# A hybrid encoder layer on one core: the router's search in a fixed order, and another issue order for everything before it

## The chip, the cores and the metric

The kernel runs on one core of a Trainium2 chip. The core has five engines that work at the same time and meet only through semaphores: TensorE (PE, matmuls; PEld is its weight load), VectorE (DVE), ScalarE (ACT), GpSimd (POOL) and SyncE (SP, which here only issues DMAs). The metric is the device time of one execution in microseconds (us), as the median of repeated runs.

## The reference

One layer of a bidirectional encoder on x of 1024 tokens x 1024 channels, in fp32. What is computed, in short:

```python
n = rms_norm(h, norm1_w)
proj = n @ w_in                                  # 1024 x (4608 conv + 2048 gate + 64 scalar) columns
c = silu(centred_dwconv(conv_in, conv_w, conv_b))  # 7 taps along the sequence
q, k, v, xs, Bm, Cm = split(c)
o_gdn = rms_norm(gated_delta_fw + gated_delta_bw) * silu(g_gate)      # 8 heads of 128, chunks of 64
y = ssd_fw + ssd_bw + D * x_ssd                  # Mamba-2 style, 16 heads of 64, 2 groups
y = rms_norm(y * silu(z))
h = h + concat([o_gdn, y]) @ w_out

n = rms_norm(h, norm2_w)
aff = softmax(n @ w_router)                      # 1024 tokens x 16 experts
vals, idx = top_k(aff.T, 128)                    # every expert chooses 128 tokens
xs = n[idx]
y = (silu(xs @ w_gate) * (xs @ w_up)) @ w_down * vals     # 16 experts, hidden width 512
h = h + scatter_add(y at idx)
out = rms_norm(h, final_norm_w)
```

## The kernel before, in words

The program is one long sequence of small jobs. Each job is a Python function that issues a few instructions on one or two engines; a job with `yield` in it is issued in pieces. Every job is entered with `at(slot, function, ...)`. `flush("mixer")` then issues the 3602 pieces of the mixer (everything up to the router's logits), in the order of a table of numbers, `ORDER["mixer"]`, and `flush("moe")` issues the experts, sorted by slot. Within an engine the instructions run in the order in which they were issued. Both flushes stand under `tc.manual_schedule()`, where that order is kept. The block of code between them, which holds the router's choice of tokens, does not: there a scheduler decides the order, and it may put an instruction of this block among those of the mixer or of the experts.

Matmuls of fp32 data are made from three passes: each operand is split into a high part (a rounded copy, made on ACT) and the rest (a subtraction, on DVE), and hi x hi, hi x lo and lo x hi are added up in PSUM. In the rows `whi` and `wlo` are the two parts of a projection weight, and `n` is a tile of activations or of output weights.

The stages, in order of time:
- RMSNorm and transposes of x, up to about 40 us. ACT copies the transposed x, scaled by a column of gains, out of PSUM (`n<-g,cols`); DVE makes the rest. `Rf` is a small tile in which the decay rates of the heads are prepared with an Exp.
- The input projection in units of 128 columns (`w_unit`, L242; `w_half`, L250), with the convolution of each unit, and under it the 8 gated-delta heads (DVE, POOL and ACT beside PE).
- The two SSD groups, about 770 to 940 us: per head a decay matrix E is made, POOL subtracts (`E<-E,tb_gc`) and masks it (L560), ACT takes its Exp, DVE multiplies it, POOL adds up and PE uses it (L1118). `xw` is an input that is weighted on POOL.
- The output projection in 6 rounds (L1289). At the end of a round `o_end` adds the product to the residual on DVE (`n<-pj,n`).
- The router's logits (L1326, L1335), which end in `lg` on DVE.
- The choice of tokens, in the block under no manual schedule. Softmax: Exp of `lg` on ACT, sum and reciprocal on DVE, `aff`. Then 15 rounds that fix the 128th largest affinity of every expert, two bits a round: DVE compares all affinities with three trial thresholds (`msk<-aff,trial`), PE counts them with a matrix of ones (`c`, L1533), DVE picks the largest threshold that still has at least 128 (`best`, L126, then L1537) and makes the next trials. Then the positions of the chosen tokens (L1543 to L1565), and per expert eight one-hot tiles (`oh`, job `rt`), from which PE collects the token numbers and their weights (`aux`, L1580); POOL issues the gather of the expert's 128 rows (`place<-n2D,idx`, L1591).
- In the gaps of the 15 rounds the first expert's six weight tiles are split: ACT makes the high parts (`place<-place`, six at once), DVE the rests, 12 halves of 128 x 512.
- 16 experts (`L1648`, `L1664`, `L1667`, `L1612`), their weights streamed from HBM through a pool of buffers; a tail with the final norm.

An Exp and a Silu belong to different function tables of ACT. `warm` is a 128 x 1 dummy on which the kernel calls a function early, so that its table (`ACT_TABLE_LOAD`) is there when it is needed: an Exp of `warm` in the last output round, and a Silu of `warm` right behind the Exp of `lg` in the source.

Of the kernel before, what the change touches and what calls it, by code (L numbers as in the profile page):

```python
# [55 lines left out]
        "7Qg}c3kPK`5*ET@QA{06FP5FyI*nce!$cry87zb0dO2uqG-|6y=#e_C9-@Z|aim`iONHeSSC7*1bbOsaJ3UTM&>3|?ok*{M6);+pPAt!?gz=*A"
        "dKIjKF?zgS4I#|YNpw;jUMJII^>V#TuYrl8<a#Yk(i!wRSO+O|N?|3eg%x_T^y^`zUZrR0^)N+G)f4pw*Z|Y?CfEeiHS2P^tSFVvrB~}2dZykC"
        "X=QV^o~<(rIrK)IMQ77%^jf*uC~ScZdXvtov+H#_r=F)f>-jpJUZ6v6wm@#ZS#Oay=GJ+Hj(V<MsPpRbdc8iOE9iW3UZfZ6PI6kJkLazsu->M("
        ">m543E~pDgUq}}bP6<WzQk_Zf(p_~oeN=bXU4&!$xK6K&>Eikjl+b5%DV<vAA*VCCq?}9Z0;Y^U3<XV3-Ak9zm342?QK+JK>m!iQ9EFN9k3wZ#"
        "MOW3;^c8(xyt>dwpVfP$tFF)K8p1_gN#{5DO)XtZ_tiD^1!-#Qf~JhADbHNedvzgG*zA+8j!;_{F-1*1y<Z>DJM~H7pgygOnd0WOuBYqkL;A9Q"  # L60
        "sjo_^D_qmp^$mSf-_j*aDO1`s&><>m>gz_PvAM19=)1bCX{7Jz`}&P;s1NH#;^oW({ZN-Tk96Z870fGL(LB~qbQ9sJZW^SS(8N?T)y;F=)RZ;N"
        "bqG)OGyPtF)6ew_UCF%Ae@qMALbuctOl4EWw9?IFzqxs@Kj{zpqpo49nii&|X=PgKw&t^LC7WM#dh=F))iG6TUCY!q-}QIhTDQ?PO-=Jd|Ik16"
        "UpciC(i&xc>3|8CP^PsGWq#|n!XMpU|I=+uYx7!C2MuP3sbks(Q#+$gdpUQ|{q#F+3>s@fn+~R<31jM-dZxZ1(@*!;VNE*YO()aYbTQ7bX<!<f"
        "0cK#Z9VTQn1M~nL-efZ2g$QPl86iGU57Z+h4K@)?B$GiHX-1juX0#b2T57_X%qEL$Wi=junQZ2_Y(<vc?Bd-_6!Ed*(Zq9@uBL~HDml98DSJ^("
        "PDw+B#U_UE&-60AO)T@*tPt;G#+mVEqM2kAM#9)8gvn-#nQ8zv{*~V*BB90TCZ^EWOf%EX3=_vV>}O`0S!TB6cqXo4oMYyShr;+64-;TK6F*33"
        "41<g1ex8|c7MK7AFd;_4geHUp!V<GkSY*OtBFTv`9EO*a*hIi(CMrh7#F*IhmvclcgR4yvOp2S#YV*=0HAzHkOk_-n$uKfT!z3n|u-2?I>*Xf7"
        "u)%B;Phno0l;Ww(F|*P{$5m#tu*D?Dlp#HCG26{nv(4<3jnqO6Ok>iRRJhyhFuTki6BC!4)Ob{$-edNeG?MnpeJ<gZ*>4J90nBX<m{^zxV`ChQ"
        "i)rzQd1DTlbeJCVVkSIj4x7B@h{=HY@Rd1kGGi9ZYu=i7rVySs@6GApJR{^0^2)P2ut<<?_`#er`SGLqB=fxaEc#-KVlga%7t94y9M6jmVOBhA"
        "zM4y>Bn}tfj@vOCUN)D_F5HcKa4()PC*|(4$&NYjl(}Ngnw*#mOW{tuXwHf6!^3#RTr;JyEMCBCrkuQ|JXXMpSV=Z2<9<AV*Ufd48?Ty!SOu$M"
        "HOwf_TsJq&G3joY!gvI$V-37zZsARHTjp&eQ>cl@@dVz%lUNIDV;!uE1+g$574Dde*g*WQxhK@cdU#jvPT~EK2Jg$fZyw-7Y=Wn;5iZ3?_`p0g"  # L70
        "&9OP2!L!&9&tnT|+Q~Z}nMbBRKE+meQQEt*^;l?$t+76~!M505xP(tkQ|usq8K0RB*cCftN9->7x#@(B@i7j>=Vl;w!H1?B_P{5iLHNQ9!hhHk"
        "ui#_z)cnC_I9Sfl@HxJ~<@f`iO8dg}!rs_NcE6c^conbVbsU1<%u9TQeX&2@z-4$-Gyq>?7drso;2#_=ti%xl+MhTIf8l#vC37@>H$Q~oxEhDy"
        "P&tng*5C@^r}>Rw!LF6|rx}Oi<n$IhS!es%@$y&rJNzI&l2GzUVI8i=4YFtDzO!_(ZEU*{C*VgMD|EKq>;#-7OvK69)lL?lh@bE;cDGZ|+s~-%"
        "7bMFzV0%at%7(VnWN#`?!=83JPQ`@wD}KZ2@<cD&+s?o~c7W|`!`QGkoDFXy*v7WMFvt#;?HM==huDZVl8tPm*lAYTs5Y97W2f6uHi3<9W7wF&"
        "Oq^k7;Y^&3L+xygW#`~PJJ1f3Ia}J%cC?*`^Kh;()6T_Ic9tD(N7&gmv5hNAX6IuPQA4``N7^}du1zW_xm|=~>{vU`e#iNeQ`nR?wQP+QPb0*$"
        "8Etwy&W^VW>_WT9F2=<e$ELOEY+hjr=Ck>1W}CrgvRQ;3b|Egr#lg7*<J%>6f}Loa*gSTU>~6v)c9+d>m)b-&o1{H<vdwOD*iE<@x7ckqtDRzV"
# [1757 lines left out]
```

## Time and profile before

| | |
|---|---|
| runs | 1676.93, 1672.53 and 1685.21 us, median 1676.93 |
| profiled execution | 1671.89 us; span of its trace 1670.2 us |
| mean granted TensorE clock | 0.972 |
| PE busy | 1550.8 us (93%) |
| DVE busy | 1211.5 us (73%) |
| ACT busy | 982.0 us (59%) |
| POOL busy | 730.0 us (44%) |
| DMA | 254.20 MB, mean 152 GB/s |

The profiled execution is 5.0 us below the median of the runs, and 0.6 us below the lowest of them. Busy shares are means over stages that differ: PE is near its limit in the projections, POOL in the SSD stage, DVE in the router's rounds, and the DMA engines in most of the experts' stage.

### The profile page before, as it was taken

How to read it: one execution, taken by the hardware profiler on the slowest of the kernel's cores; microseconds unless marked ns; L12 is line 12 of the kernel's file. 1: busy time of each engine (PE TensorE's matmuls, PEld its weight loads, DVE VectorE, ACT ScalarE, POOL GpSimd, SP SyncE). 2: the span in 40 equal slices, each digit the busy share in tenths (PEclk: the TensorE clock that was granted, in tenths of full speed). 3: DMA queues.
4: the chain of work that ended last, by engine and by line, in shares of the span. 5: the costliest groups of instructions: out<-in, count | busy, mean ns of one | idle time of the engine just before them, and what ended most of it. 6: DMA issues, size and time to landing. Idle time of an engine off the chain costs nothing. (4 is left out here: it accounts for less than half of the span.)

```text
span 1670.2 us, 23559 instructions
## 1 busy us (share of the span) xinstructions
PE 1550.8 (93%) x8290; PEld 1264.7 (76%) x8290; DVE 1211.5 (73%) x2045; ACT 982.0 (59%) x1788; POOL 730.0 (44%) x533
## 2 busy tenths in 40 slices
PE   5989999999999999998989999998996499899997
PEld 4768888888889888887765687687885377677774
DVE  4686768686767677757779976864556598789875
ACT  5476485858586767465542574243455177677764
POOL 1285263647454654425898877713032011111112
PEclk9999999999999999999999999999997599999999
DMA  4322223223231322222332245457787289999955
GB/s 137 98 60 43 45 65 68 75 56 87 42 98 28 105 70 63 39 70 95 108 101 70 67 135 172 150 183 263 256 284 291 111 311 372 329 382 375 389 184 213
DMA packets 174784, 254.20 MB, mean 152 GB/s; under 512 B 54370, under 2 KB 112027, under 8 KB 174667
## 3 DMA queue, kind: packets, MB, share of 16 engines
q1 hardware_dynamic: 170202, 236.45, 42.3%
q0 software_dynamic: 4464, 16.25, 3.8%
q8 instruction: 65, 1.06, 0.3%
q14 instruction: 53, 0.43, 0.1%
HBM read 221.01 MB, written 31.65 MB: 151 GB/s over the span
## 5 line engine op out<-in xcount | busy, mean ns | idle before, releaser
L242 PE MATMUL pj<-n,whi 128*128 128x512 f32 x1664 | 482.5, 412 | 9.8 <-ACT whi L129 7.5
L242 PEld LDWEIGHTS pj<-n,whi 128*128 128x128 f32 x1664 | 301.0, 190 | 79.2 <-ACT whi L129 11.1
L242 PE MATMUL pj<-n,wlo 128*128 128x512 f32 x832 | 263.4, 398 | 3.6 <-DVE wlo L123 3.5
L123 DVE TENSOR_TENSOR place<-place 128x1024 fp32r<-128x1024 f32 (+1 forms) x182 | 208.0, 1184 | 27.8 <-ACT place L129 27.8
L126 DVE SCALAR_TENSOR_TENSOR cacc<-pj,cols,cacc 128x1023 f32<-128x1023 f32 (+2 forms) x156 | 199.3, 1278 | 22.8 <-POOL cacc L123 20.1
L123 POOL TENSOR_TENSOR cacc<-cacc,cpr 128x1021 f32<-128x1021 f32 x60 | 145.7, 2429 | 153.4 <-ACT cacc L129 81.0
L1648 PE MATMUL pj<-place 128*128 128x512 f32 x768 | 198.3, 410 | 2.0 <-DVE place L123 1.3
L129 ACT ACTIVATE place<-place 128x1024 fp32r<-128x1024 f32 (+1 forms) x181 | 181.5, 1053 | 16.8 <-issue 8.5
L242 PEld LDWEIGHTS pj<-n,wlo 128*128 128x128 f32 x832 | 156.2, 189 | 45.8 <-DVE wlo L123 8.3
L1648 PEld LDWEIGHTS pj<-place 128*128 128x128 f32 x768 | 144.5, 192 | 40.6 <-DVE place L123 5.3
L123 DVE TENSOR_TENSOR n<-n 128x1024 fp32r<-128x1024 f32 x64 | 84.3, 1327 | 68.9 <-ACT n L129 40.7
L1591 POOL DMA_INDIRECT place<-n2D,idx x16 | 17.4, 1088 | 259.4 <-ACT place L129 93.7
L129 ACT ACTIVATE n<-n 128x1024 fp32r<-128x1024 f32 x64 | 66.7, 1056 | 104.1 <-DMA n<-in_w_out_dram 55.2
L123 DVE TENSOR_TENSOR wlo<-wraw,whi 128x512 fp32r<-128x512 f32 x106 | 96.7, 914 | 15.0 <-ACT whi L129 14.9
L1289 PE MATMUL pj<-n 128*128 128x512 f32 x384 | 97.4, 408 | 4.1 <-DVE n L123 4.1
L129 ACT ACTIVATE whi<-wraw 128x512 fp32r<-128x512 f32 x106 | 65.8, 625 | 57.7 <-PE pj L242 47.5
L129 ACT ACTIVATE place<-g 128x512 fp32r<-128x512 f32 (+1 forms) x48 | 26.9, 561 | 110.4 <-PE g L1612 106.2
L1289 PEld LDWEIGHTS pj<-n 128*128 128x128 f32 x384 | 72.5, 191 | 24.2 <-DVE n L123 5.8
L129 ACT ACTIVATE cpr<-pj,cols 128x1021 f32<-128x1021 f32 x60 | 66.5, 1109 | 26.6 <-PE pj L242 16.9
L129 ACT ACTIVATE u<-c,bt 128x128 f32<-128x128 f32 x128 | 39.6, 363 | 60.1 <-DVE ud L123 58.4
L123 POOL TENSOR_TENSOR ex<-N,nm 128x512 f32<-128x512 f32 x48 | 62.2, 1304 | 14.6 <-PE g L785 9.9
L123 DVE TENSOR_TENSOR E<-E,tb_dt 128x1024 f32<-128x1024 f32 x32 | 56.9, 1790 | 15.5 <-ACT E L129 15.3
(328 smaller groups left out, 3202.9 us busy)
## 6 DMA issues: line engine op xcount, KB each, us to landing
place<-in_w_gate_dram SPq DMA_DIRECT2D x64, 512.0 KB, 9.3
place<-in_w_up_dram SPq DMA_DIRECT2D x64, 512.0 KB, 8.7
place<-in_w_down_dram SPq DMA_DIRECT2D x64, 512.0 KB, 9.8
wraw<-in_w_in_dram SPq DMA_DIRECT2D x106, 256.0 KB, 3.3
E<-rowsD SPq DMA_DIRECT2D x32, 512.0 KB, 3.8
n<-mixD SPq DMA_DIRECT2D x64, 256.0 KB, 3.4
n<-in_w_out_dram SPq DMA_DIRECT2D x64, 256.0 KB, 4.4
dec<-rowsD SPq DMA_DIRECT2D x16, 512.0 KB, 7.7
```

The costliest lines, as they stand in the source:

```text
L123: eng.tensor_tensor(o, a, b, op=op)
L126: V.scalar_tensor_tensor(o, a, s, b, op0=op0, op1=op1, **kw)
L129: S.activation(o, i, f, **kw)
L242: T.matmul(pj[c0][:, hs], lhsT=w[:, d % 4, :], rhs=nn[d][:, hs], start=(d == 0 and a == 0), stop=(d == ND - 1 and a == 2))
L1289: T.matmul(wst["po", r][t], lhsT=m[:, 0, ts], rhs=w[:, 1, :], start=(k == k0 and a == 0), stop=(k == k1 - 1 and a == 2))
L1591: nc.gpsimd.indirect_dma_start(out=ex["xs", e], out_offset=None, in_=n2D[:, :], in_offset=ex["idx", e])
L1648: T.matmul(po, lhsT=xT[:, j, d % 4, :], rhs=wt[k][:, HALF[dd]], start=(d == 0 and a == 0), stop=(d == ND - 1 and a == 2))
```

## The change

Two things are changed.

First, the table `ORDER["mixer"]` is another one. It has the same 3602 numbers, and 3313 of them stand at another place, most of them 1 to 10 places from where they were. One line of it stands for all in the diff.

Second, the block between the two flushes now stands under `tc.manual_schedule()`, so that each engine runs it in the order of the code. With that, the code is put in another order: the split of the affinities into three bf16 parts (`aux` 2 to 4, `res`) moves from behind the positions into rounds 0 and 1; the 12 halves of the rests stand one in each of rounds 2 to 13; `rt` of the first two experts waits 0.5 instead of 6.0 slots between its one-hots and its matmuls, and expert 1 starts at slot -28.1 instead of -29, behind expert 0's.

The diff, with changes of indentation alone left out:

```diff
 ORDER = {
     "mixer":
-        "K-56Az<YW2ga0MGm%YEiosW{g`+q)qAVwf&;HOuC4|4kGfBVn=j}R*mJMh=X38+BaK)k^J0VCBi?*",
+        "<irO!(E=a+XaC3l#FO3!9T5<L+5Wfx?*D=4ff#|9fmngqfjEJ<fj>T8;D6dIGVc",
...
+    with tc.manual_schedule():
     act(lg, lg, AF.Exp)
     act(warm, mhalf[:, :1], AF.Silu)
     den = hp.tile([128, NT], F32, name="den")
...
     V.memset(best[0][:, 0, :], 0.0)
     V.tensor_copy(trial, over3(tv["digit"][:, 0, :]))
+        res = hp.tile(SE, F32, name="res")
     for j in range(15):
         tt(V, msk3, aff[:, :, None, :].to_broadcast(S4), trialf[:, None].to_broadcast(S4), OP.is_ge)
-        if j > 1 and halves:
+            if j < 2:
+                src = res if j else aff
+                V.tensor_copy(aux[:, :, :, 2 + j], src)
+                tt(V, aux[:, :, :, 4] if j else res, src, aux[:, :, :, 2 + j], OP.subtract)
+            elif halves:
             rest(*halves.popleft())
         pc = ctile([128, 3, NE])
...
     stt(posx, sel, -512.0, posx, OP.mult, OP.add)
-    res = hp.tile(SE, F32, name="res")
-    V.tensor_copy(aux[:, :, :, 2], aff)
-    tt(V, res, aff, aux[:, :, :, 2], OP.subtract)
-    V.tensor_copy(aux[:, :, :, 3], res)
-    tt(V, aux[:, :, :, 4], res, aux[:, :, :, 3], OP.subtract)

     def rt(e):
         oh = mp.tile([128, NT, 128], BF, name="oh", tag="oh")
         for t in range(NT):
             V.tensor_scalar(oh[:, t, :], slots, posx[:, t, e:e + 1], None, op0=OP.is_equal)
-        yield 6.0
+        yield 0.5 if e < 2 else 6.0
         pa = ctile([128, 8])
...
     at(-30, rt, 0)
-    at(-29, rt, 1)
+    at(-28.1, rt, 1)
```

**The start, on ACT.** ACT's queue around 41 us, where `n<-g,cols` are the last copies of x and `Rf<-Rf 128x48` is the Exp of the SSD decay rates, whose data come by a DMA. Before:

```order
L129 ACTIVATE whi<-wraw 128x512
L129 ACTIVATE n<-g,cols 128x512 x9
L129 ACTIVATE Rf<-Rf 128x48
L129 ACTIVATE whi<-wraw 128x512
L129 ACTIVATE n<-g,cols 128x512 x2
L129 ACTIVATE O<-pj 128x1024
```

and in the change:

```order
L129 ACTIVATE n<-g,cols 128x512 x9
L129 ACTIVATE whi<-wraw 128x512
L129 ACTIVATE O<-pj 128x1024
L129 ACTIVATE whi<-wraw 128x512
L129 ACT_TABLE_LOAD
L129 ACTIVATE tb_beta<-qd 128x128
L129 ACT_TABLE_LOAD
L129 ACTIVATE Rf<-Rf 128x384
L129 ACTIVATE whi<-wraw 128x512
L129 ACTIVATE Rf<-Rf 128x48
```

The Exp stood ahead of two of the copies of x, and stands now behind all of them and behind the first product's way out of PSUM (`O<-pj`).

**The output rounds and the start of the search, on DVE.** DVE's queue in the fifth output round, where the scheduler had put the search's first two instructions (L1525, L1526) ahead of the additions of `o_end` (`n<-pj,n`). Before:

```order
L1224 TENSOR_SCALAR Y<-Y,ry 128x512 x8
L123 TENSOR_TENSOR n<-n 128x1024 x8
L1525 MEMSET best_11578 128x16
L1526 COPY trial<-digit 128x48
L123 TENSOR_TENSOR n<-pj,n 128x512 x4
L123 TENSOR_TENSOR n<-n 128x1024 x4
```

and in the change, some 50 rows later, behind the logits:

```order
L123 TENSOR_TENSOR lg<-lg,r_121 128x64
L1490 TENSOR_REDUCE den<-lg 128x8
L1491 RECIPROCAL den<-den 128x8
L123 TENSOR_TENSOR aff<-lg,den 128x128
L1526 MEMSET best_11580 128x16
L1527 COPY trial<-digit 128x48
L123 TENSOR_TENSOR msk_11579<-aff,trial 128x384
L1533 CAST aux<-aff 128x128
L123 TENSOR_TENSOR res<-aff,aux 128x128
```

The two now wait for nothing that is late, and stand between `aff` and the first comparison.

**The rounds and the Exp before them, on DVE and ACT.** DVE in round 3 and the beginning of round 4 before, where `place<-place` is a half of a rest:

```order
L123 TENSOR_TENSOR trial<-best_11578,digit 128x48
L123 TENSOR_TENSOR msk_11577<-aff,trial 128x384
L123 TENSOR_TENSOR place<-place 128x512
L126 SCALAR_TENSOR_TENSOR best_11578<-c,trial 128x48
L123 TENSOR_TENSOR place<-place 128x512
L1537 TENSOR_REDUCE best_11579<-best_11578 128x16
L123 TENSOR_TENSOR place<-place 128x512
L123 TENSOR_TENSOR trial<-best_11579,digit 128x48
L123 TENSOR_TENSOR place<-place 128x512
L123 TENSOR_TENSOR msk_11577<-aff,trial 128x384
```

and in the change:

```order
L123 TENSOR_TENSOR trial<-best_11580,digit 128x48
L123 TENSOR_TENSOR msk_11579<-aff,trial 128x384
L123 TENSOR_TENSOR place<-place 128x512
L126 SCALAR_TENSOR_TENSOR best_11580<-c,trial 128x48
L1543 TENSOR_REDUCE best_11581<-best_11580 128x16
L123 TENSOR_TENSOR trial<-best_11581,digit 128x48
```

Three rounds had four halves each, behind every one of their steps; now a round has one, in the place where DVE waits for PE's count. On ACT the Exp of `lg` stood behind a table load, since the scheduler had put the Silu of `warm` ahead of it into the last output round:

```order
L129 ACTIVATE n<-n,r_121 128x1024 x3
L129 ACT_TABLE_LOAD
L129 ACTIVATE lg<-lg 128x128
L129 ACTIVATE place<-place 128x1024 x6
L129 ACTIVATE place<-g 128x512 x2
```

and in the change:

```order
L129 ACTIVATE n<-n,r_121 128x1024 x3
L129 ACTIVATE lg<-lg 128x128
L129 ACT_TABLE_LOAD
L129 ACTIVATE warm<-mhalf 128x1
L129 ACTIVATE place<-place 128x1024 x6
```

The load now follows the Exp. Elsewhere the table moves instructions by a few places. Two of these moves are on POOL in the SSD stage: `xw<-xk,tb_wst` stood behind the first and the second pair of `E<-E,tb_gc` and mask after 803 us, and both now stand ahead of the first pair.

## Rows read from the trace of the kernel before

**Rows 1.** Windows: length, busy us by engine, granted clock, DMA share, GB/s.

```profile
780.00:940.00 160.00, 145.84 (x634) 106.08 (x633) 133.69 (x113) 70.06 (x80) 144.78 (x78) 0.97 0.28 88
1290.00:1300.00 10.00, 2.01 (x32) 1.48 (x32) 7.90 (x24) 0.00 (x0) 0.00 (x0) 0.50 1.03 422
1300.00:1320.00 20.00, 7.52 (x81) 5.31 (x81) 13.48 (x56) 0.00 (x0) 0.00 (x0) 0.50 0.08 33
1400.00:1600.00 200.00, 194.17 (x917) 150.57 (x917) 173.37 (x274) 142.85 (x173) 29.12 (x20) 0.98 1.01 372
```

**Rows 2.** Timeline of ACT at the start: start, us, instruction, idle before and releaser.

```profile
41.05 0.24 ACT L129 ACTIVATE Rf<-Rf 128x48 f32<-128x48 f32 x1 [6.53 <-DMA Rf<-in_ssd_A_log_dram]
```

**Rows 3.** Timeline of PE at the start.

```profile
42.44 0.50 PE L250 MATMUL pj<-n,whi 128*128 128x512 f32 x1 [3.56 <-ACT n L129]
43.38 0.62 PE L250 MATMUL pj<-n,whi 128*128 128x512 f32 x1 [0.43 <-DVE n L126]
```

**Rows 4.** Timeline of DVE in the fifth output round.

```profile
1137.50 0.20 DVE L1526 COPY trial<-digit 128x48 int32<-128x48 int32 x1 [3.52 <-POOL digit L1473]
1137.62 2.47 DVE L123 TENSOR_TENSOR n<-pj,n 128x512 f32<-128x512 f32 x4
```

**Rows 5.** Timeline of PE in the fifth output round.

```profile
1133.47 2.79 PE L1289 MATMUL pj<-n 128*128 128x512 f32 x11 [0.27 <-DVE n L123]
1138.95 3.51 PE L1289 MATMUL pj<-n 128*128 128x512 f32 x8 [2.70 <-DVE n L123]
```

**Rows 6.** Timeline of ACT at the logits.

```profile
1277.22 1.28 ACT L129 ACT_TABLE_LOAD   x1
1278.51 0.31 ACT L129 ACTIVATE lg<-lg 128x128 f32<-128x128 f32 x1
```

**Rows 7.** Timeline of DVE in the search and the positions.

```profile
1277.01 0.23 DVE L123 TENSOR_TENSOR lg<-lg,r 128x64 f32<-128x64 f32 x1
...
1279.74 0.56 DVE L123 TENSOR_TENSOR msk<-aff,trial 128x384 bf16<-128x384 f32 x1
...
1281.32 0.52 DVE L123 TENSOR_TENSOR aux<-res,aux 128x128 bf16<-128x128 f32 x1
...
1284.04 0.56 DVE L123 TENSOR_TENSOR msk<-aff,trial 128x384 bf16<-128x384 f32 x1
1284.52 0.68 DVE L123 TENSOR_TENSOR place<-place 128x512 fp32r<-128x512 f32 x1
1285.20 0.21 DVE L126 SCALAR_TENSOR_TENSOR best<-c,trial 128x48 f32<-128x48 f32 x1
...
1296.05 0.56 DVE L123 TENSOR_TENSOR msk<-aff,trial 128x384 bf16<-128x384 f32 x1
1297.21 0.21 DVE L126 SCALAR_TENSOR_TENSOR best<-c,trial 128x48 f32<-128x48 f32 x1 [0.60 <-PE c L1533]
...
1311.52 0.56 DVE L123 TENSOR_TENSOR msk<-aff,trial 128x384 bf16<-128x384 f32 x1
...
1316.98 2.69 DVE L1576 TENSOR_SCALAR oh<-slots,posx 128x128 bf16<-128x128 bf16 x16
```

**Rows 8.** Timeline of POOL at the gather.

```profile
1320.83 1.25 POOL L1591 DMA_INDIRECT place<-n2D,idx  x1 [45.66 <-DVE ax L123]
```

**Rows 9.** Timeline of PE behind the gather and in the experts.

```profile
1325.39 1.98 PE L1612 MATMUL g<-ident,place 128*128 128x128 f32 x8 [5.46 <-DMA place<-n2D,idx]
...
1427.95 1.12 PE L1612 MATMUL g<-ident,ga 128*128 128x128 f32 x4 [5.36 <-DVE ga L123]
```

**Rows 10.** Timeline of PE in the SSD stage.

```profile
784.85 2.07 PE L242 MATMUL pj<-n,whi 128*128 128x512 f32 x4 [2.89 <-ACT whi L129]
...
876.82 2.08 PE L242 MATMUL pj<-n,whi 128*128 128x512 f32 x4 [4.60 <-ACT whi L129]
```

**Rows 11.** Timeline of POOL in the SSD stage.

```profile
803.55 1.99 POOL L123 TENSOR_TENSOR E<-E,tb_gc 128x1024 f32<-128x1024 f32 x1 [1.48 <-DMA E<-rowsD]
...
807.55 1.47 POOL L123 TENSOR_TENSOR xw<-xk,tb_wst 128x512 f32<-128x512 f32 x1
```

More of the change, by code (lines that the diff above doesn't have):

```diff
@@ L73 @@
[L73 to L76, printed above, removed]
-        "*_<}F>`%4J>~g!`uCQBeVcW>Awp+20Z7N>a7O>6a**&(o+!V1HT_L*#TiBxFMdZGiEoQgdyl$`EC*1*gM@w7K7PqVHLE(@+Y}d$XrEO(f+Y&aD"
@@ L1485, in trunk @@
     aff, ones_b, before_b, slots, aux, posx, lg = (tv[n] for n in ("aff", "ones_b", "before_b", "slots", "aux", "posx", "lg"))
-    act(lg, lg, AF.Exp)
-    act(warm, mhalf[:, :1], AF.Silu)
-    den = hp.tile([128, NT], F32, name="den")
-    V.tensor_reduce(den, lg, axis=AX.X, op=OP.add)
-    V.reciprocal(den, den)
-    tt(V, aff, lg, den[:, :, None].to_broadcast(SE), OP.mult)
-    mp = pool("mp")
-    ex = {}
-    halves = deque()
-    def split(w, e, i):
-        raw = eraw.pop(epos[w, e, i])
-        if (w, i) in WHOLE:
-            ex["w", w, e, i] = raw,
-            return None
-        hi, lo = take(F32R), take(F32R)
-        ex["w", w, e, i] = hi, lo
-        act(hi, raw, AF.Copy)
-        return raw, hi, lo
@@ L1507, in rest @@
-    def rest(parts, cols, last):
-        raw, hi, lo = parts
-        tt(V, lo[:, cols], raw[:, cols], hi.bitcast(F32)[:, cols], OP.subtract)
-        if last:
-            give(raw)
-    EARLY = [(w, 0, i) for w in range(2) for i in range(3)]
-    for key in EARLY:
-        parts = split(*key)
-        halves.extend((parts, HALF[h], h) for h in range(2))
-    msk3 = hp.tile([128, NT, 3, NE], BF, name="msk3")
-    best = [hp.tile([128, 4, NE], F32, name=f"best{i}") for i in range(2)]
-    trial = hp.tile([128, 3, NE], I32, name="trial")
@@ L1541, in trunk @@
-    ge = hp.tile([128, NT + 1, 2, NE], BF, name="ge")
-    gt, eq = ge[:, 1:, 0, :], ge[:, 1:, 1, :]
-    P.memset(ge[:, 0], 0.0)
-    thr_b = thr[:, None, :].to_broadcast(SE)
-    tt(V, gt, aff, thr_b, OP.is_gt)
-    tt(V, eq, aff, thr_b, OP.is_equal)
-    gf = ge.rearrange("p t k e -> p t (k e)")
-    pb = gtile([128, NT + 1, 2 * NE])
-    T.matmul(pb, lhsT=ones_b, rhs=gf, start=True, stop=False)
-    T.matmul(pb[:, :NT], lhsT=before_b, rhs=gf[:, 1:], start=False, stop=False)
-    for u in range(1, NT):
-        T.matmul(pb[:, u + 1:], lhsT=ones_b, rhs=gf[:, 1:NT + 1 - u], start=False, stop=(u == NT - 1))
@@ L1553, in trunk @@
-    b_gt, b_eq = pb[:, :NT, :NE], pb[:, :NT, NE:]
-    need = hp.tile([128, 2, NE], F32, name="need")
-    V.tensor_scalar(need[:, 0], pb[:, NT, :NE], -1.0, 128.0, op0=OP.mult, op1=OP.add)
-    V.tensor_scalar(need[:, 1], need[:, 0], 512.0, None, op0=OP.add)
-    needb = lambda i: need[:, i, :][:, None, :].to_broadcast(SE)
-    over = hp.tile(SE, F32, name="over")
-    sel = hp.tile(SE, BF, name="sel")
-    tt(V, over, b_eq, needb(0), OP.subtract)
-    stt(sel, over, 0.0, eq, OP.is_lt, OP.mult)
```

210 lines of the change are left out of this document (133 added, 77 removed).

## The prediction

> **What bounds the kernel now.** I read the windows first. Over the whole span PE is busy 93% of the time, so a piece of the mixer is worth only what PE idles there. The windows show where another engine sets the pace [rows 1]: POOL in the SSD stage (144.78 of 160 us, with PE at 145.84), DVE in the search (7.90 of 10 us, PE only 2.01, at the lower clock, 0.50), and the DMA engines beside PE in the experts (a share of 1.01 over 200 us). In the search nothing else runs: what its chain loses, the span loses.
>
> Then I went through the timeline of PE for its idle time, and at each hole to the engine that ended it. In the mixer four of its holes after 40 us are over 2.5 us: 3.56 us at 42.44 [rows 3], 2.89 at 784.85 and 4.60 at 876.82 [rows 10], 2.70 at 1138.95 [rows 5]. Last came the chain from the logits to the first gather: the logits are ready at 1277.01 + 0.23 = 1277.24 [rows 7], the gather of the first expert is issued at 1320.83 [rows 8], 43.6 us later, and PE begins with the experts at 1325.39, released by that gather [rows 9].
>
> **The change, part by part.** The sum is made against the profiled execution, 1671.89 us.
>
> *The start: -4.0.* ACT idles 6.53 us for a DMA that brings the SSD decay rates, and only then runs their Exp at 41.05 [rows 2]; the last two copies of x stand behind it. PE waits for these 3.56 us, and for DVE's part of the same tile another 0.43 [rows 3]. In the new order the Exp stands behind the copies and behind the first product's way out, when its data have long landed. Nothing else kept the copies back, so both waits go: 3.56 + 0.43 = 4.0. At the least nothing is gained, if the DMA of a weight is as late; more than 4.0 is not on PE at this place. I take 4.0, since the wait has a named releaser. The Exp itself (0.24 us) moves beside PE's projection and costs nothing as long as ACT has idle time there; without that cover it costs 0.24.
>
> *The fifth output round: -1.3.* The first copy of the search's trials waited 3.52 us on DVE for constants from POOL, and the additions of `o_end` stood behind it until 1137.62 [rows 4]. PE had ended its last product at 1133.47 + 2.79 = 1136.26, and went on at 1138.95, released by DVE [rows 5]. Without the copy the additions can begin when the product ends: 1137.62 - 1136.26 = 1.36, less what a signal takes, 1.3. What is left of the 2.70 us is the additions' own time, which is late next. Bounds: 0 and 2.70.
>
> *The table load ahead of the Exp: -1.2.* The logits are ready at 1277.24; at 1277.22 ACT began to load the table of Exp, since the Silu of `warm` had driven it out, and the Exp of the logits ran at 1278.51 [rows 6]. Now the load for Silu follows the Exp. The Exp can start at about 1277.3: 1.2 less, with bounds 0 and 1.28. The load that follows takes the same 1.28 us, beside DVE's softmax; behind it on ACT are the six high parts, of which the first is needed in round 2 only, several us later.
>
> The Trainium skill, "ScalarE: Activation LUTs", section "What ACT_TABLE_LOAD costs", gives a switch of tables as 1283 ns for the load and about 1380 ns for a drain, 2.66 us in all. The load's row agrees (1.28), the drain does not show: the Exp starts 0.01 us behind the load's end. By the page this term would be -2.6, and the sum 1.4 us lower.
>
> *The search's first instructions on the path: +0.3.* The memset and the copy now stand between `aff` and the first comparison. The copy took 0.20 us [rows 4], the memset has a third of its elements; with the gap between two instructions I take 0.3 (bounds 0.2 and 0.4).
>
> *The rounds: -4.5.* From the first comparison at 1279.74 to the fifteenth at 1311.52 are 31.78 us for 14 rounds [rows 7]. A round without halves is the mean of the eight from 1296.05 to 1311.52: 15.47 / 8 = 1.93; in it DVE idles 0.60 us for PE's count. Three rounds had four halves each: from 1284.04 to 1296.05 are 12.01 us for these three and one clean round, 10.08 / 3 = 3.36 each. What a single half costs shows in the first step of round 2: comparison at 1284.04, half at 1284.52 (0.68 us), `best` at 1285.20, that is 1.16 us behind the comparison, and in the clean round from 1296.05 to 1297.21 it is 1.16 too. So one half just fills the wait, and the twelve halves, one a round, cost nothing. In round 0 a cast and a subtraction of 128 x 128 fill the same place. Round 1 ends with the subtraction into bf16, which took 0.52 us [rows 7], about 0.2 more than fits. So 14 x 1.93 + 0.2 = 27.3, and 31.78 - 27.3 = 4.5. Bounds: the halves might be hidden less well, 0.1 us in each of 12 rounds (3.3), or round 1 not at all late (4.8). DVE has no cover beyond these 0.60 us: a half that were 0.3 us longer would cost 3.6 us in all.
>
> *The first expert's positions: -0.8.* The gather waited for 16 one-hots, 2.69 us [rows 7], of two experts. Now eight stand ahead of the first expert's counts: -1.34. But PE's eight small matmuls, which ran behind the second expert's one-hots, are now waited for; a wait of that kind was 0.60 us in the rounds. I take -0.8, with bounds of -1.34 and 0 (if the gather waits for both experts as before). The second expert's index comes later by as much, and its gather stands behind the first's 1.25 us on POOL [rows 8] anyway.
>
> *From the gather to the end: nothing given back.* The DMA engines moved next to nothing from 1300 to 1320 us (share 0.08 [rows 1]): the weights that fit into the buffers had landed, and the next wait for the experts to free some. So the transfers start earlier by as much as the gather does, and the experts' stage moves as a whole. The loads of the experts themselves are the same.
>
> *The rest of the new table: 0, between -6 and +5.* Most moves are small and lie under a busy PE. In the SSD stage the weight split behind which PE stalls at 784.85 now stands ahead of two Exps that wait for POOL, while that of 876.82 still stands behind such Exps. But POOL sets the pace there, and I expect it to give a gain of 2.9 back at the next wait for it. Against that stands the move of `xw` on POOL (below).
>
> Sum: -4.0 - 1.3 - 1.2 + 0.3 - 4.5 - 0.8 = -11.5, so 1671.89 - 11.5 = 1660.4. The profiled execution stood 5.0 us below the median of the runs and 0.6 below the lowest; as the runs scatter upward from a floor, I put the floor's 0.6 on top: **1661 us**.
>
> **The rivals.**
>
> *More goes than that.* If the new order also removes the stalls of the SSD stage for good, 2.89 + 4.60 = 7.5 us [rows 10], the time is 1661 - 7.5 = 1653.5. For it: both have ACT as their releaser, whose order the table sets. Against it: ACT waits there for POOL's masks, and POOL is at 90% of the window.
>
> *The experts swallow the router's gain.* If the stage from 1340 us on is bound by the weights' transfers, and these don't start earlier, the -6.2 us of the four router terms are lost: 1667. For it: the DMA share of 1.01, and a stall of 5.36 us at 1427.95 [rows 9], where a late weight held up ACT and DVE. Against it: the idle DMA engines before the gather, whose next transfers the experts themselves release.
>
> *The start's gain is taken by the next wait,* a weight that arrives as late, or is given back before the SSD stage: 1661 + 4 = 1665.
>
> *Slower than before: POOL in the SSD stage.* Two `xw` now stand ahead of the pair that started at 803.55; before, the first of them ran at 807.55 [rows 11]. If its input is not there sooner, POOL stands still for 807.55 - 803.55 = 4.0 us, in a stage where it is the pace. One such wait makes 1665, three take the whole sum, and from four on, 1661 + 16 = 1677, the change is slower than before. For it: POOL's order has the `xw` of other heads moved as well. Against it: while POOL waits, its own earlier waits shrink, and a later place of the sums spares POOL some waits for DVE.
>
> *The change does not do what it says* is excluded for the order, which is fixed in the program; only that a half does not fit into its 0.60 us is open, and it is in the bounds.
>
> **How the numbers follow.** My forecast has 0.52, with a range of its own of 1656 to 1667 (bounds of the terms, and 5 us of the table's rest, which will not all fall on one side). The larger gain has 0.20, the experts' rival 0.10, the start's 0.09, POOL's waits 0.09, of which one or two waits have most and four or more 0.03. The range that leaves out 2 in 10 goes from 1648, the larger gain with the bounds of the terms, to 1674, two of the POOL waits (8 us) and 5 us more from the rest of the table. A measurement here can tell about 1%, 16.8 us: faster by more is below 1660.2, slower by more above 1693.7. My forecast lies on the edge, and about half of it is below: 0.25, and with the larger gain 0.45. Slower by over 1% needs eight of POOL's waits or something that no row shows: 0.03. Within 1%: 0.52.
>
> **What would show it.** In the changed profile: the ACT copies of x before 41 us, and PE without a hole there (else the start failed); PE's hole in the fifth output round near 1.4 us; the Exp of the logits right behind them, its load after; 14 rounds of 1.93, with `best` 1.16 behind each comparison (if 1.3 or more, the halves don't fit); the gather about 37.4 us behind the logits; the same length from there to the end as before, 1671.89 - 1320.83 = 351 us (if it is 6 longer, the experts swallowed it); and in the SSD stage POOL's waits for `xk`. A time above 1674 would mean that the SSD stage grew, and one under 1648 that PE's small holes all over the mixer went, which I count at nothing.

## The result and the profile after

The changed kernel took 1660.35 us (median of 4 runs, 1659.2 to 1661.73) against 1677.95 us of the kernel before (4 runs, 1672.53 to 1685.21): ratio 0.9893, 95% interval 0.9854 to 0.9932. Timed once more against other runs of before it gave 0.990 (0.988 to 0.992); one of its six runs, in a slow state, took 3914 us and is left out of that ratio. The forecast was 1661 us. The profiled execution has a span of 1657.5 us (1659.2 us in all), 12.7 less than before's.

Four stretches of the program show where the two executions part (us):

| | before | after | difference |
|---|---|---|---|
| logits ready (DVE) | 1277.24 | 1268.11 | -9.1 |
| logits to the issue of the first gather | 43.59 | 37.49 | -6.1 |
| gather to PE's first work for the experts | 4.56 | 4.52 | 0 |
| from there to the end of the span | 344.8 | 347.4 | +2.6 |

**The start.** ACT's timeline in the changed kernel (start, length, instruction, idle before and its releaser), and PE's:

```profile
35.81 1.27 ACT L129 ACTIVATE n<-g,cols 128x512 fp32r<-128x512 f32 x2 [1.15 <-PE g L359]
...
50.14 0.23 ACT L129 ACTIVATE Rf<-Rf 128x48 f32<-128x48 f32 x1
```

```profile
39.11 0.51 PE L250 MATMUL pj<-n,whi 128*128 128x512 f32 x1 [1.26 <-DVE n L126]
...
41.71 1.97 PE L471 MATMUL g<-ident,O 128*128 128x128 f32 x8 [1.16 <-ACT O L129]
```

The last of these rows, the transposes of the first product, stood in before at:

```profile
46.86 1.94 PE L471 MATMUL g<-ident,O 128*128 128x128 f32 x8 [1.16 <-issue]
```

The last two copies of x run at 35.81, six us earlier than in before (41.72), and the Exp of the decay rates stands at 50.14, beside PE's projection. PE's hole of 3.56 us [rows 3] is gone, but not both waits, as I had it: DVE's part of the tile still holds PE up for 1.26 us. The transposes of the first product start at 41.71 instead of 46.86.

**The end of the first output round.** I placed this at "the fifth output round"; by the program's jobs these additions are the first round's, and PE waits for them with the second round's products. DVE and PE in the changed kernel:

```profile
1126.26 2.65 DVE L123 TENSOR_TENSOR n<-pj,n 128x512 f32<-128x512 f32 x4 [1.64 <-PE pj L1289]
```

```profile
1131.33 0.50 PE L1289 MATMUL pj<-n 128*128 128x512 f32 x1 [0.62 <-ACT n L129]
1132.60 7.78 PE L1289 MATMUL pj<-n 128*128 128x512 f32 x33 [0.76 <-DVE n L123]
```

The additions now wait for PE (1.64 us), not for POOL's constants [rows 4], and PE's hole of 2.70 [rows 5] has shrunk to two of 0.62 and 0.76.

**The logits and the search.** ACT, then DVE, then POOL and PE:

```profile
1265.68 3.21 ACT L129 ACTIVATE n<-n,r 128x1024 f32<-128x1024 f32 x3
1268.80 0.29 ACT L129 ACTIVATE lg<-lg 128x128 f32<-128x128 f32 x1
1269.11 1.28 ACT L129 ACT_TABLE_LOAD   x1
```

```profile
1267.88 0.23 DVE L123 TENSOR_TENSOR lg<-lg,r 128x64 f32<-128x64 f32 x1
...
1269.68 0.29 DVE L123 TENSOR_TENSOR aff<-lg,den 128x128 f32<-128x128 f32 x1
...
1270.13 0.56 DVE L123 TENSOR_TENSOR msk<-aff,trial 128x384 bf16<-128x384 f32 x1
...
1274.02 0.56 DVE L123 TENSOR_TENSOR msk<-aff,trial 128x384 bf16<-128x384 f32 x1
1274.49 0.69 DVE L123 TENSOR_TENSOR place<-place 128x512 fp32r<-128x512 f32 x1
1275.17 0.21 DVE L126 SCALAR_TENSOR_TENSOR best<-c,trial 128x48 f32<-128x48 f32 x1
...
1297.21 0.56 DVE L123 TENSOR_TENSOR msk<-aff,trial 128x384 bf16<-128x384 f32 x1
...
1302.67 1.39 DVE L1577 TENSOR_SCALAR oh<-slots,posx 128x128 bf16<-128x128 bf16 x8
...
1304.62 0.35 DVE L123 TENSOR_TENSOR ax<-ax 128x1 f32<-128x1 f32 x2
```

```profile
1305.60 1.25 POOL L1592 DMA_INDIRECT place<-n2D,idx  x1 [38.34 <-DVE oh L1577]
```

```profile
1310.12 1.13 PE L1613 MATMUL g<-ident,place 128*128 128x128 f32 x4 [3.56 <-DMA place<-n2D,idx]
```

The table load [rows 6] stands behind the Exp. Fourteen rounds take 1297.21 - 1270.13 = 27.08 us, against 31.78 [rows 7]; in round 2 the half runs from 1274.49 and `best` comes 1.15 us behind its comparison, so it fills the wait and nothing more. Eight one-hots stand ahead of the gather. From the first one-hot to the gather are 2.93 us, where before had 1320.83 - 1316.98 = 3.85.

**The SSD stage.** My rival for a slower kernel was POOL's wait for `xw`:

```profile
795.88 2.29 POOL L123 TENSOR_TENSOR xw<-xk,tb_wst 128x512 f32<-128x512 f32 x2 [1.83 <-DMA E<-rowsD]
```

```profile
828.46 2.15 PE L1118 MATMUL c<-xk,E 128*128 128x64 f32 x16 [2.43 <-DVE E L123]
...
867.79 2.08 PE L1168 MATMUL c<-xw,Bt 128*128 128x512 f32 x2 [5.49 <-DVE hs L123]
```

POOL does both `xw` at 795.88 after 1.83 us of idle time, about what it had waited before (1.48 [rows 11]): their input was ready, and the 4.0 us of the rival did not come. PE's stall at 784.85 [rows 10] is gone, but a new one of 2.43 us, for DVE, stands at 828.46, and the one of 4.60 us is back as 5.49 at 867.79, with another releaser. PE itself now waits 1.40 us at 837.66 for an `xw` of POOL (2.9 us at this place in `table_only`, `packed` and `late_rt`), a cost that the sum did not have. Over the whole stage next to nothing is won: POOL's first `E<-E,tb_gc` starts 6.9 us earlier than in before (769.27 against 776.18), its first behind 940 us 7.2 (939.61 against 946.81).

**The tail.** PE by windows, the same stretch of work in both kernels (columns: length, busy us by engine, granted clock, DMA share, GB/s), first before, then after:

```profile
1619.00:1649.00 30.00, 27.37 (x113) 19.88 (x114) 13.63 (x17) 11.98 (x16) 1.55 (x1) 1.00 0.47 157
```

```profile
1603.60:1633.60 30.00, 27.65 (x104) 20.33 (x105) 11.75 (x14) 11.64 (x16) 1.55 (x1) 0.89 0.41 134
```

The two holes behind which this stretch lies are the same in both, 1.85 and 1.70 us. In the execution of before the granted clock stayed up (1.00); in that of after it fell twice to the lower level (mean 0.89), and the tail took 2.6 us longer. Everything from the gather to 1600 us is as long as before, to 0.2 us.

### The profile page after: what moved, and what is told of

It is laid out like the page before. It is cut to its first block, busy times and chain, and to the rows that moved or that the text cites. A ratio compares the mean times of both kernels' runs of the same rounds, so it can differ in the third digit from the quotient of the medians.

```text
span 1657.5 us, 23558 instructions
## 1 busy us (share of the span) xinstructions
PE 1547.7 (93%) x8290; PEld 1266.2 (76%) x8290; DVE 1214.4 (73%) x2045; ACT 976.0 (59%) x1784; POOL 730.3 (44%) x533
## 5 line engine op out<-in xcount | busy, mean ns | idle before, releaser
L123 DVE TENSOR_TENSOR wlo<-wraw,whi 128x512 fp32r<-128x512 f32 x106 | 103.0, 974 | 26.1 <-ACT whi L129 25.9
L123 POOL TENSOR_TENSOR E<-E,tb_gc 128x1024 f32<-128x1024 f32 x32 | 66.2, 2068 | 7.7 <-DMA E<-rowsD 7.7
```

Source lines behind the costliest of these rows:

```text
L123: eng.tensor_tensor(o, a, b, op=op)
```

## The experiments

`rates_only`, `packed`, `silu_first`, `late_rt` and `before_again` were executed once each (1674.4, 1666.8, 1672.3, 1660.2 and 1683.7 us), so only stretches of them are compared.

**The table alone, and the search alone.** `table_only` is the kernel before with the new table; `search_only` is the changed kernel with the old one.

```diff
 table_only:  before, with ORDER["mixer"] of the changed kernel
 search_only: changed kernel, with ORDER["mixer"] of before
```

> The kernel before with the new table alone; the search stays under the scheduler. My theory, that the parts add up: the logits are ready 9.1 us earlier less the 1.3 us of the fifth output round, where the scheduler's copy of the trials can still stand in front of the additions, so between 7.5 and 9.1 us before 1277.2; from the logits to the first gather 43.6 us as before; the span about 1662 us (1670.2 - 8), a ratio near 0.995. Rival, that the table only pays together with the fixed search: logits less than 4 us earlier, a ratio of 0.998 or more.

Measured: ratio 0.9955 (0.9938 to 0.9973, 12 runs), 1670.0 us. The logits come at 1269.82, the search takes 43.59. So the table pays by itself, by 7.4 us up to the logits of this execution, just under the 7.5 to 9.1 that I had expected, and by 7.5 between the medians.

> The changed kernel with the old table: only the search is fixed. My theory: PE's hole of 3.56 us at 42.4 us stays, the hole of 2.70 us in the fifth output round falls to about 1.4, the logits are ready 1.3 us earlier than 1277.2, and the gather is issued 37.5 us behind them instead of 43.6. The span is 1670.2 - 7.4 = 1662.8 if the experts' stage keeps its length of before, and up to 2.7 us more if TensorE's clock falls in the last experts as it did in the changed kernel; a ratio near 0.996. Rival, that part of the 6.1 us comes from the new table (other loads in flight, another state of the buffers): from the logits to the gather 40 us or more.

Measured: ratio 0.9933 (0.9909 to 0.9958), 1665.8 us in the median of 6 runs, 11 us less, where I had expected 7.4. The profiled execution is one of the two longest (1670.0 us), and its logits come at 1281.99, 4.7 us later than in before's and not 1.3 earlier: near 295 us alone it loses 5 us on before's, with a granted clock of 0.70 from 285 to 300 us where that has 1.00. What it shows are single stretches. From the logits to the gather are 36.87 us, 6.7 less than before; the further 0.6 against the changed kernel's profile is ACT, which had done its last norms in time (there the Exp waited for them, 1268.11 to 1268.80). PE's hole behind the first output round is 1.38 us, as the sum had it:

```profile
1146.16 11.17 PE L1289 MATMUL pj<-n 128*128 128x512 f32 x48 [1.38 <-DVE n L123]
```

But between the matmuls 5700 and 6150, counted from the program's start, this execution wins 3.6 us on before's, not 1.3: 1.3 at the hole, 1.6 in the ten matmuls behind it, and 0.7 at 1162.43, where before waits 0.54 us for DVE and this execution does not. Behind the hole of 2.70 us the clock had fallen in before, and here it did not, which makes the 1.6. By windows, before and `search_only`:

```profile
1136.00:1160.00 24.00, 21.30 (x89) 17.23 (x88) 12.25 (x15) 9.03 (x14) 13.93 (x63) 0.93 0.63 198
```

```profile
1140.00:1164.00 24.00, 22.36 (x102) 18.06 (x101) 13.38 (x15) 10.30 (x16) 18.07 (x69) 1.00 0.74 242
```

**One job of the start.** `rates_only` moves that Exp alone in the kernel before; `rates_back` puts it back in the changed one, ahead of the last copy of x.

```diff
 # rates_only, in flush("mixer"); job 55 is the preparation of the rates
+seq = seq[:106] + seq[108:142] + [55, 55] + seq[142:]
 # rates_back
+seq = seq[:113] + [55, 55] + [i for i in seq[113:] if i != 55]
```

> The kernel before with one job moved: the Exp of the SSD decay rates (and its negation) issued behind the last copies of x and the first product. My theory: PE's hole of 3.56 us at 42.4 us falls under 1 us, the sixth matmul unit of the projection starts 4 to 5 us earlier, and this lasts to the logits, about 1273 instead of 1277.2. Rival, that POOL gives the pace again in the SSD stage and takes it back: logits at 1276 or later.

```profile
42.26 0.50 PE L252 MATMUL pj<-n,whi 128*128 128x512 f32 x1 [0.92 <-DVE n L126]
...
44.86 1.09 PE L473 MATMUL g<-ident,O 128*128 128x128 f32 x8 [1.16 <-ACT O L129]
...
42.00:52.00 10.00, 8.58 (x40) 6.79 (x41) 6.55 (x10) 5.71 (x8) 1.19 (x4) 1.00 0.21 55
```

PE's hole falls to 0.92 us, and the clock stays up behind it (1.00 from 42 to 52 us). From 51 us on the execution is 3.5 to 3.65 ahead of before's at the same matmul, a little less than expected. That lasts to 205 us; from there to 238 it loses 2.3 behind two falls of the clock (before's has one there), and from 785 to 790, in the SSD stage, another 1.4 (granted clock 0.72 from 780 to 792, where the same stretch of before has 0.86). At the logits 0.5 is left (1276.71; I had expected about 1273). So most of what was lost again stands behind falls of the clock; whether POOL's pace would have taken it anyway, as the rival has it, one execution does not tell.

> The changed kernel with the Exp of the SSD decay rates (and its negation) put back ahead of the last copy of x. My theory, that this one job makes most of the start's gain: PE waits again 3 to 4 us before the unit of the last copies, the clock falls behind it, and the product's way out begins about 4 us later than in the changed kernel's two profiles (41.2 and 41.7), at 45 to 46; with the other moves of the start kept, it stays 1 us or more ahead of the kernel before (46.9 and 48.2). Rival, that the other moves of the first 40 us make the gain and the Exp's data would be there by now: under 43.

```profile
41.72 1.58 PE L252 MATMUL pj<-n,whi 128*128 128x512 f32 x2 [2.35 <-ACT n L129]
...
44.89 1.94 PE L473 MATMUL g<-ident,O 128*128 128x128 f32 x8 [1.16 <-issue]
...
40.00:50.00 10.00, 7.12 (x19) 5.20 (x20) 4.43 (x10) 6.28 (x9) 0.00 (x0) 0.50 0.25 70
```

The wait for ACT is back (2.35 us, less than the 3 to 4 that I had expected), with the clock at the lower level behind it, and the product leaves at 44.89, 3.2 and 3.7 us later than in the two profiles of the changed kernel: just under what I had expected, and 2.0 to 3.3 us ahead of before. So the place of the Exp makes more than half of the start's gain, other moves the rest. Ratio 0.9922 (0.9896 to 0.9947): against the 0.990 of the changed kernel not clear of it.

**The halves.** `packed` puts them back four to a round.

```diff
-            elif halves:
+            elif j < 5:
                 rest(*halves.popleft())
...
+            if 1 < j < 5:     # behind best, behind the reduction, behind the trials
+                rest(*halves.popleft())
```

> The changed kernel with the twelve halves four to a round in rounds 2, 3 and 4, one behind each step, as the scheduler had them before. My theory: these three rounds take 3.36 us each and the other nine 1.93, so the gather is issued 3 x 1.43 = 4.3 us later, 41.8 us behind the logits instead of 37.5. Rival, that the long rounds of before came from ACT, whose high parts were not ready: then the three rounds take what ACT needs, under 3 us, or the rounds' sum stays within 1 us of 27.1.

```profile
1279.81 0.56 DVE L123 TENSOR_TENSOR msk<-aff,trial 128x384 bf16<-128x384 f32 x1
...
1289.89 0.55 DVE L123 TENSOR_TENSOR msk<-aff,trial 128x384 bf16<-128x384 f32 x1
...
1291.82 0.56 DVE L123 TENSOR_TENSOR msk<-aff,trial 128x384 bf16<-128x384 f32 x1
```

Three rounds take 1289.89 - 1279.81 = 10.08, 3.36 us each, then 1.93 again; 14 rounds take 31.37 us, 4.3 more than in the changed kernel. From the logits to the gather are 41.15 us: 4.3 above the 36.87 of the executions where ACT was not late. ACT's high parts, the rival, were not what these rounds waited for.

**The table load.** `silu_first` brings back the load between the last norms and the Exp.

```diff
-        act(lg, lg, AF.Exp)
         act(warm, mhalf[:, :1], AF.Silu)
+        act(lg, lg, AF.Exp)
```

> The changed kernel with the two lines on ACT swapped, Silu of warm ahead of the Exp of the logits; in the program the Silu then comes before the last norms, so that one table load for Exp stands between these and the Exp, as before. My theory: the load's 1.28 us are on the path, logits to aff in 2.2 us (before 2.17) instead of 1.57 in the changed kernel's profile; the gather 38.1 us behind the logits. Rival, the Trainium skill's page ScalarE: Activation LUTs, which counts a drain of 1.38 us with each load: logits to aff in 3.5 us or more.

```profile
1280.71 1.28 ACT L129 ACT_TABLE_LOAD   x1
1282.01 0.31 ACT L129 ACTIVATE lg<-lg 128x128 f32<-128x128 f32 x1
```

```profile
1280.51 0.23 DVE L123 TENSOR_TENSOR lg<-lg,r 128x64 f32<-128x64 f32 x1
...
1282.91 0.29 DVE L123 TENSOR_TENSOR aff<-lg,den 128x128 f32<-128x128 f32 x1
```

The logits are ready at 1280.51 + 0.23 = 1280.74 and `aff` starts at 1282.91, 2.17 us later as in before, where `search_only` took 0.94. The load costs 1.23 us, the gather comes 38.09 us behind the logits. The Exp starts 0.02 us behind the load's end.

The Trainium skill ("ScalarE: Activation LUTs", "What ACT_TABLE_LOAD costs") counts about 1380 ns of drain with each switch of tables; here no row shows it.

**The positions.** `late_rt` has `yield 6.0` and slot -29 again.

> The changed kernel with the first two experts' positions as before: both sets of one-hots ahead of the first counts. My theory: from the first one-hot to the gather 3.85 us as before, instead of 2.93, the gather 38.4 us behind the logits instead of 37.5, PE's start with the experts as much later. Rival, that the gather waits for both experts' indices anyway: no difference.

```profile
1304.92 2.69 DVE L1577 TENSOR_SCALAR oh<-slots,posx 128x128 bf16<-128x128 bf16 x16
...
1308.78 1.25 POOL L1592 DMA_INDIRECT place<-n2D,idx  x1 [40.26 <-DVE ax L123]
```

From the first one-hot to the gather are 1308.78 - 1304.92 = 3.86 us, from the logits 37.79: 0.92 more than the 36.87 without ACT's lateness. The gather waits for its own expert only.

**The changed kernel again.**

> The changed kernel itself, once more. My theory: what differs between executions of one program is TensorE's clock, which falls behind PE's holes in some executions and not in others; the search is the same in each. So: from the logits to the gather 37.5 us within 0.7 again, the fifteen rounds 27.1, the experts' stage 344.8 us where the clock does not fall in its last 70 us and up to 3 us more where it does, the logits anywhere from 1267 to 1275. The ratio about 0.990 (0.985 to 0.994). Rival, that the 2.6 us given back in the experts belong to the change: 347 us again in this stage.

The search took 36.87, the rounds 27.09; the logits came at 1267.1. The experts' stage took 347.4 again, with the clock down at the same two places. But it took 344.9 and 345.1 in `packed` and `late_rt`, and 347.3 in the second profile of before, again with falls behind the two holes of the tail, and 347.9 in `rates_only`, with falls elsewhere in the stage: the longer stage occurs with either kernel, so it does not belong to the change.

This execution also shows that a higher clock can bring nothing. Its clock did not fall at the start (nor in `late_rt` and `spin`), as it did in the first profile of the changed kernel, and at PE's 130th matmul it is 2.05 us ahead of that (43.80 against 45.85). Then comes a wait that the first profile does not have:

```profile
58.77 1.53 PE L510 MATMUL g<-Rf 128*128 128x384 f32 x4 [2.44 <-DVE Rf L123]
```

Behind it the execution is 0.6 us later than the first. DVE's rows tell why; this execution, DVE and POOL, then DVE in the first profile:

```profile
55.92 2.70 DVE L123 TENSOR_TENSOR Rf<-Rf 128x384 f32<-128x384 f32 x1
```

```profile
55.87 2.34 POOL L123 TENSOR_TENSOR cacc<-cacc,cpr 128x1021 f32<-128x1021 f32 x1 [15.49 <-ACT cpr L129]
```

```profile
56.69 0.55 DVE L123 TENSOR_TENSOR Rf<-Rf 128x384 f32<-128x384 f32 x1
```

The same instruction of DVE takes 2.70 us where POOL has begun an addition 0.05 us before it, and 0.55 in the first profile, where POOL begins 1.2 us behind it (57.92). In `late_rt` and `spin` POOL also begins just before it, and it takes 2.70 and 2.72 us; in `packed` and `silu_first` POOL begins later, and it takes 0.55. PE, ahead by 2 us, let ACT and with it POOL begin so much earlier, and the gain was lost in the wait for DVE.

**Throwaway matmuls.** `spin` fills four of PE's holes in the experts' stage, to hold the clock up.

```diff
+    def spin(n):
+        pd = gtile([128, 512])
+        for _ in range(n):
+            T.matmul(pd[:, :384], lhsT=ones_b, rhs=msk3.rearrange("p t k e -> p (t k e)"), start=True, stop=True)
...
+        if e == 1: spin(12)      # behind the counts in rt
...
+        if e in SPIN: spin(SPIN[e])     # in ht; SPIN = {4: 24, 14: 6, 15: 6}
```

> The changed kernel with 48 throwaway matmuls (128 x 384, bf16, results not read) in four of PE's holes of the experts' stage: 12 while the first gather is under way, 24 in the hole of 5.4 us before the fifth expert's transposes of ga, 6 in each of the last two such holes. My theory, that the clock is what these holes cost beyond themselves: the granted clock is up when the first expert begins or within 2 us, instead of 4.7 us later (-1.5 to -2.3 us), does not fall at the fifth (-2.3), nor in the tail; the experts' stage takes about 340.5 us instead of 344.8 to 347.4, the median is about 4 to 6 us below the changed kernel's. Rival, that from 1340 to 1410 us the weights' transfers set the pace, so that the first gain is given back before the fifth expert: 342 to 343 us.

```profile
1309.89 4.00 PE L1579 MATMUL g<-msk,ones_b 128*128 128x384 bf16 x12
1313.69 1.94 PE L1622 MATMUL g<-ident,place 128*128 128x128 f32 x8
...
1416.66 0.65 PE L1622 MATMUL g<-ident,ga 128*128 128x128 f32 x4 [2.81 <-DVE ga L123]
```

Ratio 0.9904 (0.9882 to 0.9925): no gain on the changed kernel. The experts' stage took 345.2 us, not 340.5. The clock was up 2 us behind the first expert's begin, but the fifth expert's transposes start 1416.66 - 1313.69 = 103.0 us behind PE's first work, as in the changed kernel (1412.77 - 1310.12 = 102.7): the gain was given back by then, as the rival said. With the DMA engines at a share of 1.01 from 1340 to 1410 us in this execution, as in the changed kernel's, that speaks for the weights as its pace, but no run changes the transfers. At the fifth expert 2.81 us of the hole were left and the clock fell still (0.89 from 1410 to 1425 us; 0.77 from 1408 to 1423 in the changed kernel), where I had expected no fall. In the tail the clock held (1.00 from 1603 to 1640), but so it did without dummies in `packed`, whose stage is about as long (344.9).

**The holes' clock.** `before_spin` does the same in the two holes of the kernel before, and `before_again` is that kernel once more.

```diff
     def w_half(c0, h, d):
+        if (h, d) == (1, 6): spin(24)
...
     def o_mm(r, k):
+        if (r, k) == (1, 0): spin(16)
```

> The kernel before with throwaway matmuls (128 x 128, results not read) in the two holes of PE that the change removes: 24 ahead of the unit that waits at 42.4 us, 16 ahead of the output product that waits at 1138.9 us. The waits themselves stay. My theory, that these holes cost the clock as well: the granted clock no longer falls at 43.6 and at 1139.3, the product's way out at 46.9 us comes 1 to 2.5 us earlier though its copies come no earlier, and 10 us behind the second hole another 1 to 1.7 us are saved; ratio about 0.998. Rival, that the clock falls there by chance as elsewhere in the mixer, or that the holes cost only their length: no gain at either place.

> The kernel before, profiled once more. My theory, that the clock's falls make the executions of the mixer differ and those behind the two long holes come each time: the clock falls again at 42 to 44 us and at 1139 (shifted by what went before), elsewhere at other places; the logits between 1275 and 1285 us; the search 43.6 us and the rounds 31.8 again. Rival, that one execution is like the other: logits at 1277.2 within 0.5, and the same falls.

By windows, 42 to 52 us, in this order: before, its second profile, `before_spin`:

```profile
42.00:52.00 10.00, 7.97 (x25) 5.97 (x26) 5.03 (x11) 5.92 (x8) 0.00 (x0) 0.66 0.09 27
```

```profile
42.00:52.00 10.00, 7.08 (x19) 5.20 (x20) 4.75 (x13) 6.08 (x9) 0.00 (x0) 0.52 0.10 26
```

```profile
42.00:52.00 10.00, 8.84 (x57) 7.57 (x56) 5.72 (x15) 6.59 (x9) 0.00 (x0) 1.00 0.10 28
```

At the start the clock stayed up (1.00 against 0.66 and 0.52). The dummies ran too long, 5.5 us, so the transposes of the product started 0.6 us later than in before's first profile, and not 1 to 2.5 earlier as expected. The next hole that all have is a wait for a weight's rest on DVE; before, then `before_spin`:

```profile
123.47 0.73 PE L242 MATMUL pj<-n,wlo 128*128 128x512 f32 x2 [2.15 <-DVE wlo L123]
```

```profile
122.44 0.73 PE L242 MATMUL pj<-n,wlo 128*128 128x512 f32 x2 [2.18 <-DVE wlo L123]
```

From the transposes to the end of this wait are 123.47 - 46.86 = 76.6 us in before, 77.0 in its second profile, but 122.44 - 47.48 = 75.0 in `before_spin` and 119.94 - 44.86 = 75.1 in `rates_only`, the two executions whose clock stayed up. So behind the transposes the lower clock cost 1.6 us in one execution of before and 2.0 in the other. Ahead of them, from the matmul behind DVE's wait (43.38 [rows 3]), before took 3.48 us and `rates_only` 2.60 (42.26 to 44.86): 0.9 more, and 1.1 in the second profile. In all the clock behind this hole cost about 2.5 and 3 us.

At the second hole the experiment failed: the dummies ran at 1106.09, where PE was busy, and not in the hole (2.73 us are still there), and the clock fell (0.93 from 1136 to 1160). The kernel as a whole is slower, ratio 1.0038 (1.0017 to 1.0058), 6.9 us between the medians. The dummies at 1106.09 took 3.74 us of PE's time; the rest I leave open.

The second profile of before is at the other end of its runs, 1683.7 us, with the logits at 1286.54, 9.3 later than the first at one and the same program; the search is 43.58. Of that, 5.3 us come in one stretch near 1220, by windows:

```profile
1215.00:1235.00 20.00, 19.63 (x93) 17.24 (x92) 7.97 (x12) 10.31 (x16) 5.53 (x5) 0.74 0.58 202
```

## Why the prediction was right, and where it was not

**The median was right, the working was half of the reason.** The sum was -11.5 us from an execution that stood 5.0 us below the median of the runs, and I put 0.6 us on top for the floor. The medians lie 17.6 us apart. Had I counted from the median, I should have said 1665.4. So two errors of about 5 us met: a base that was low by chance, and terms that were too small. That the number was hit to 1 us is luck. Nor is there a floor at 1672.5, as I took it: later runs of before went down to 1668.5.

**The search: right, term by term.** Expected -6.2 for the four terms and measured -6.1 in the changed kernel's profile: the table load -0.6 there (ACT's norms were late) and -1.23 in `search_only` and `silu_first` (said: -1.2); the first instructions +0.12 (0.3); the rounds -4.70 (-4.5), `packed` gives 4.3 of them back; the positions -0.92 (-0.8), `late_rt` gives them back. Where ACT was not late, the whole took 36.85 to 36.87 us in four executions (`search_only`, `after_again`, `spin`, `rates_back`), 6.7 less than before.

**The start: right in the mechanism, too small.** The step that did not hold is "nothing else kept the copies back, so both waits go": DVE's part of the tile still costs 1.26 us, so of -4.0 the waits gave 3.56 + 0.43 - 1.26 = 2.7. The rest of the new order of the first 40 us brought the hole itself 1.0 earlier (37.85 instead of 38.88), and another 0.5 by one matmul that now runs ahead of it. The last 0.9 is the clock: from the matmul behind DVE's wait to the transposes before took 3.48 us and the changed kernel 2.60 (39.11 to 41.71). That makes 5.15 in all to the first product's transposes. The term that I did not have was the clock: I had the hole's length as its price. The granted clock from 40 to 54 us tells the same for all profiles: 0.63 to 0.76 in the four that have the hole and nothing in it (both of before, `search_only`, `rates_back`), 1.00 in the two where it is filled or gone (`before_spin`, `rates_only`), and 0.88 or 1.00 in the other seven, which have the new order.

**The first output round: the hole right (1.4 left, measured 1.38), the price too small.** 1.3 was said, 3.6 is what `search_only` won there over before's execution: 1.6 of it since the clock fell behind the hole in before, 0.7 at a wait that came later. It fell there in all four profiles that have this hole (both of before, `rates_only`, `before_spin`), and not in `search_only`. It can fall there behind less: `rates_back` has a fall at this place behind holes of 1.24 and 0.76 us, while the other six profiles of the changed order with the fixed search, with holes of 0.35 to 1.19 and 0.76, have none.

**The rest of the table: zero, as far as can be seen.** POOL's waits (the rival that ends slower) did not come, the SSD stalls moved and were not lost, the output rounds have two new waits for DVE (1.15 us at 1213.76 and 0.77 at 1218.05), and the experts did not swallow the router's gain: the transfers moved with the gather, and PE's stage up to 1600 us kept its length.

**What fills the gap.** By rows, the start (5.15), the first output round (3.6 in `search_only`) and the search (6.7) make 15.5 of the 17.6 us between the medians, 4 more than the sum had for them. The rest can only be estimated. The mean granted clock of each run goes with the difference between runs of one program: over 58 runs of before, from 1668.5 us at 0.974 to 1687.8 us at 0.963, the correlation is -0.90. The medians of the clock are 0.968 for before and 0.973 for nine runs of the changed kernel. At two levels, half and full, that is 2 x 0.032 x 1676 = 107 us at the lower level, against 2 x 0.027 x 1658 = 90. The shorter search takes some 8 of these 17 us (58 us at the lower level in before's profile, 48 and 51 in the two of after); the other 9, where PE sets the pace, cost half of themselves, 4 to 5 us, at the most, since a later wait can take it back. This is an estimate, but it is the size of what the sum lacks: 17.6 - 11.5 = 6. Over three profiles with the old table (before twice, and `search_only`, whose first output round is already shorter) the logits come at 1281.9 in the mean; over seven with the new one (all but `rates_back`) at 1271.9; ten less, and 6.7 for the search make 16.7. Single executions scatter over 9 us and more on either side, so this mean is rough. Which of the falls elsewhere belong to the order of the table, and which to chance, stays open: the same program gave logits at 1268.11 and at 1274.53 (changed kernel and `packed`, alike up to there).

## What to carry to other kernels

A hole in a busy PE may cost more than its length: look at the granted clock of the stretch behind it, and add what the lower level takes there (here about 2.5 and 3 us behind a hole of 3.56, 1.6 behind one of 2.70). It is not always lost: a later wait can take it anyway. A sum against one profiled execution should be put against the median of the runs, and a stretch that no other engine disturbs (here the search) is the place where a sum of rows can be trusted to tenths of a us. Work that is to hide in a wait must be cut to the wait's length and given one to each; a scheduler that packs it made three rounds nearly twice as long.

## What was unexpected of the hardware

Executions of one program, with the same instructions in the same order, differ by 9.3 us ahead of the search (the two profiles of before), and they part at single places at which the granted clock falls in one and not in the other: in `silu_first` 8.7 us were lost before 225 us against the changed kernel, which has the same instructions up to there, with a granted clock of 0.74 from 140 to 160 us where the other has 1.00:

```profile
140.00:160.00 20.00, 19.18 (x97) 16.79 (x95) 10.71 (x16) 8.84 (x17) 11.97 (x11) 0.74 0.11 31
```

```profile
140.00:160.00 20.00, 20.00 (x121) 17.52 (x120) 13.15 (x26) 13.19 (x29) 13.04 (x11) 1.00 0.13 35
```

From 46 us up to this fall PE had no hole over 1.03 us, and 0.82 us was the last. At the gather, POOL's issue follows the end of DVE's preparation by 0.63 us in both kernels (1304.97 to 1305.60 in the changed one).
